# Attention layer: order of the value products, of the gate tiles' products, and of each attention tile's norm

## The chip, the cores and the metric

The kernel runs on one core of a Trainium2 chip. The metric is the device time of one execution in microseconds (us). Engines are named as in the profile: PE is TensorE (matmul), PEld its weight load, DVE is VectorE, ACT is ScalarE, POOL is GpSimd, SP the engine that issues most of the DMAs.

## The reference

One layer over 512 latent tokens and 256 context tokens, width 1024, in float32. Cut to what matters:

```
mod = silu(c) @ w_ada + b_ada                       # shifts, scales and gates, also for the context
h   = rms_norm(x) * (1 + sc1) + sh1                 # latent; hc likewise for the context
aq, ak, av, dq, dk, dv, dz, da, db, ga, gd = split_cols(h @ w_in)
q_a = axial_rope(rms_norm(heads(aq, 8), q_norm_g))  # 8 query heads, 2 key/value heads, 64 wide
k_a = axial_rope(rms_norm(heads(ak, 2), k_norm_g))
y_attn = softmax over (keys within 128 positions, all context keys, a sink logit) @ values
y_dn = gated DeltaNet in both directions, chunks of 64: a triangular solve per chunk, a scan over chunks
y = sigmoid(ga) * (y_attn @ w_br_attn) + sigmoid(gd) * (y_dn @ w_br_dn)
x = x + gt1 * (y @ w_out)
x = x + gt2 * (relu(norm2(x) @ w_mlp1) ** 2 @ w_mlp2)
```

## The kernel before

**Split products.** Every float32 operand of a large product is split into an upper part ("hi", rounded to fp32r) and a lower part ("lo", the rest). A product is the sum of three: hi x hi, hi x lo, lo x hi. A weight tile is 128 x 1024. `wload` fetches it into a buffer `wr` (four of them, DMA issued by SP at L250), makes `wh` with an ACT copy (L259) and `wl` in one of two ways: as a DVE subtract `wr - wh` (L266), or, with `late=True`, as an ACT copy of `-wh` (L263) followed by a DMA from POOL that adds the weight tile in memory to it (L264). There are two `wh` and two `wl` buffers, so a tile's `wh` can be written once the tile two before has had its last product with it. The queue `wq` lists the tiles in the order in which they are needed and `wnext()` hands out the next, loading one ahead.

**Order of the work.** The kernel is written with Python generators: `weave` takes steps from several of them in turn, by given shares. A scheduler then fixes one order of instructions for each engine ahead of the run; it may move an instruction past others that it doesn't depend on. During the run each engine works through its own row in order and waits by semaphores. Products accumulate in eight PSUM banks.

**Stages of this case.** Times in brackets are from the trace.

- *Attention tiles* (about 95 to 147 us). `attn_in` makes the tiles K, Q0, Q1, Q2, V, Q3. `in_tile_steps` multiplies: 16 products with `wh` (L424), for K and V another 16 of 256 columns for the context, then 8 with `wl` (L429), in steps of two k-tiles. When a tile is done it is finished: for K and Q `qk_norm` squares it (ACT L447), copies it (ACT L448), sums the squares by a product with a block matrix (PE L450), rotates (DVE L453 to L456), scales (L461), and the result is split (ACT L184, DVE L185; for K L485, L486). For V the tile is copied (ACT L495), transposed by PE (L499) and split. Woven with it are the first triangular solves: products L777, L802, L803, DVE operations L801 to L857, ACT copies L148.
- *Outputs* (185 to 295). `outputs` runs once for each query block and key/value head: for pairs of key blocks the probabilities are transposed on PE (L596), split into hi (ACT L184) and lo (DVE L185), and `values` multiplies them by the values on PE (L586), ended by ACT L610, DVE L611 and L618. `scores` runs ahead for later units: products L541 to L553, the maximum (DVE L554, L555) and the exponential (ACT L148). The remaining DeltaNet tiles (L424, L429, convolution L641 to L643) and the first three gate tiles (`ND1 = 3`, tiles `T_GD`) fill in.
- *Scans* (375 to 475, and some at 295 to 375). The DeltaNet scan over chunks is a chain of short products (PE L1152, L1164, L1185) and DVE operations (L1156, L1157, L1170, L1201). The remaining gate tiles (17) fill in: `gate_tiles` issues 24 products each (L1028), in groups of three for each k-tile: two with `wh`, one with `wl`. A gate ends with a tanh (ACT L148) and, for some, DVE L1033. DVE also has L1094 (another weight product), L1278, L1279 and L1285 (from the join of the solves) there.
- *The rest*: modulation and norms before 80 us, the output projection to 560 us, the MLP from 560 to 909 us (L317 to L319).

`combine` (L869) joins two half solves; it is called with a function that runs filling products between its two groups of matmuls.

Of the kernel before, what the change touches and what calls it, by code (L numbers as in the profile page):

```python
# [99 lines left out]
def tile_layer(ctx: ExitStack, tc: tile.TileContext, I: dict, out: bass.AP, dbg=None):  # L100
# [272 lines left out]
    for b in [wab_, xs_, cs_, rstd, scb]:  # L373
# [6 lines left out]
                                                        *range(T_DQ, T_DQ + 4))]  # L380
    wq += [(I["win"][t + i], KT) for t, i in gates[:ND1]]
    wq += [(I["wbr"][0, ct], 4) for ct in range(8)] + [(I["win"][t + i], KT) for t, i in gates[ND1:]]
# [92 lines left out]

    def k_attn():

        acc = yield from in_tile_steps(T_AK, True)
        t = qk_norm(acc[:, :512], SEQ, kg, True)
        t2 = qk_norm(acc[:, 512:768], CTX, kg)  # L480
        acc.free()
        for src, o in ((t[:, :512], slice(0, 512)), (t2[:, :CTX], slice(512, 768))):
            for kv, r in enumerate(own):
                for r2 in own:
                    A.activation(r32(KH[kv][r2, o]), src[r], AF.Copy)  # L485
                V.tensor_tensor(r32(KLo[kv][r, o]), src[r], KH[kv][r, o], op=ALU.subtract)  # L486
        t.free()
        t2.free()
        yield

    def v_attn():

        acc = yield from in_tile_steps(T_AV, True)
        raw = alloc(768)
# [11 lines left out]
        pt.free()  # L506
        yield

    def q_attn(j):
        acc = yield from in_tile_steps(T_AQ + j, False)  # L510
        t = qk_norm(acc.ap, SEQ, qgs, True)
        acc.free()
        src = t[:, :512].rearrange("p (b t) -> p b t", b=4)
        for kv, r in enumerate(own):
            split(src[r], Q[kv][r, :, j, :], Q[kv][own[1 - kv], :, j, :])
        t.free()
        yield

# [54 lines left out]
    def outputs(qb, kv):  # L573
# [7 lines left out]
        def values(at, ph, last):  # L581
            m = len(at)
            for x, i in enumerate(at):
                v = r32(VS[:, cols[i] * 256 + kv * P:cols[i] * 256 + (kv + 1) * P])
                for y, b in enumerate(ph):
                    PE.matmul(pv.ap, v, r32(b[:, x * 512:x * 512 + 512]), start=(i == y == 0),  # L586
# [281 lines left out]

    def combine(nto, XTf, XRf, XTb, XRb, XAf, XAb, inplace, between=lambda: None):  # L869

# [9 lines left out]
        Y.free()  # L880
        between()
        XO = bank()
# [8 lines left out]
        if not inplace:  # L891
            A.activation(XAf[:, :, :HC], XTf, AF.Copy)
            A.activation(XAb[:, :, :HC], XTb, AF.Copy)
        for a in range(2):
            lo, hi = quad(a, 0), quad(a, 1)
            A.activation(XAf[hi, :, HC:], XTf[hi], AF.Copy)
# [39 lines left out]
    def attn_in():  # L936
        yield from k_attn()
        for j in range(3):
            yield from q_attn(j)
        yield from v_attn()  # L940
        yield from q_attn(3)

# [61 lines left out]
    def combine0():  # L1004
# [7 lines left out]
        na, sw = v3(nat.ap), v3(swp.ap)  # L1012
        combine(NTO[0], na[:, :16], sw[:, :16], sw[:, 16:], na[:, 16:], v64(XA[0][0].ap), v64(XA[0][1].ap), False)
        nat.free()
# [6 lines left out]
    def gate_tiles(todo):  # L1021

        for kind, i in todo:
            w = wnext()
            acc = bank()
            for k in range(KT):
                for p, (x, y) in enumerate(((0, 0), (0, 1), (1, 0))):
                    PE.matmul(acc.ap, w[x][:, k, :], hx[k][y], start=(k == p == 0), stop=(k == KT - 1 and p == 2))  # L1028
                    yield
            if kind == T_GA:  # L1030
# [24 lines left out]
    for n, u in enumerate(units):  # L1055
        work = [(outputs(*u), (span(u[0])[2] + 3) // 2 + 1), (qts, QTS[n]), (inv, INV[3])]
        if n == CO:
            work.append((seq(combine0), 1))
        weave(*work, (ahead, 4))
# [198 lines left out]
    for g in range(2):  # L1258
        ms = slice(16 * g, 16 * g + 16)
        f, b = xa[0][:, ms], xa[1][:, ms]  # L1260
        run_fill(FILL[1] - CPAUSE)
        combine(NTO[1 + g], f[:, :, :HC], xr3[0][:, ms], b[:, :, :HC], xr3[1][:, ms], f, b, True, lambda: run_fill(CPAUSE))
        NTO[1 + g].free()
# [323 lines left out]
```

## Time and profile before

| | |
|---|---|
| median of 3 runs | 912.52 us (911.92 to 914.22) |
| profiled execution | 911.22 us, span 909.5 us |
| granted TensorE clock | 1.0 |
| busy: PE, PEld | 879.4, 704.7 us |
| busy: DVE, ACT, POOL | 585.4, 454.9, 25.2 us |

Each row of a timeline gives the start, the duration, the engine, the line and operation, what it writes and reads, and in brackets the idle time before it with what ended it. "ACT m L495" as a releaser is the ACT instruction of line L495 that wrote a tile m. A group row gives the busy time and the mean of one in ns, then the idle time of the engine in front of the group. Matmuls overlap, so the time from one start to the next, not the duration, is what a product takes of PE.

### The profile page before, as it was taken

What the parts mean: (1) busy time and instruction counts of PE and PEld (TensorE: products, weight loads), DVE (VectorE), ACT (ScalarE), POOL (GpSimd) and SP (SyncE); (2) the same over time, 40 slices, a digit from 0 to 9 for tenths busy, and PEclk for the clock granted to TensorE, in tenths of its full rate; (3) what the DMA queues carried; (4) which work ended last, traced back from release to release, by engine and by line L of the source; (5) the groups of instructions that cost most, each with busy time, mean ns of one, the idle gap of its engine ahead of it and who ended that gap; (6) DMA issues with size and microseconds to landing.
All of it is one profiled execution on the core that took longest, in us unless ns stands there. A gap on an engine that the chain in (4) does not pass through costs nothing.

```text
span 909.5 us, 16844 instructions
## 1 busy us (share of the span) xinstructions
PE 879.4 (97%) x7082; PEld 704.7 (77%) x7082; DVE 585.4 (64%) x999; ACT 454.9 (50%) x819; POOL 25.2 (3%) x40
## 2 busy tenths in 40 slices
PE   8999999999899999999999999999999999999998
PEld 5668777867677787777678789888888888888886
DVE  3578799887778997677867988941654335324511
ACT  6588755476568786465663445630452134113400
POOL 0010001010000002010000000000000000000000
PEclk9999999999999999999999999999999999999999
DMA  8671455533001133633316773640553224322111
GB/s 355 262 230 21 92 117 120 112 71 58 13 13 35 56 110 94 207 98 95 117 37 219 245 245 135 227 144 1 188 157 95 70 73 150 103 69 79 38 47 46
DMA packets 30460, 105.59 MB, mean 116 GB/s; under 512 B 3760, under 2 KB 4400, under 8 KB 29360
## 3 DMA queue, kind: packets, MB, share of 16 engines
q1 hardware_dynamic: 28368, 97.18, 33.1%
q0 software_dynamic: 2016, 7.34, 5.0%
q8 instruction: 55, 0.90, 0.4%
q14 instruction: 21, 0.17, 0.1%
HBM read 102.41 MB, written 2.10 MB: 115 GB/s over the span
## 4 chain that ended last, share of the span: by engine, by line
PE 80%; DVE 10%; ACT 5%; issue 2%; DMA 1%; SPq 0%; DVEq 0%; ACTq 0%
PE banks L319 16%; PE banks L317 16%; PE banks L318 16%; PE banks L1028 9%; PE banks L424 5%; PE banks L1073 2%; PE banks L429 2%; PE banks L586 2%; PE banks L596 1%; PE banks L1164 1%; ACT m L148 1%; PE banks L662 1%; PE banks L1185 1%; PE banks L1152 1%; PE banks L210 1%
## 5 line engine op out<-in xcount | busy, mean ns | idle before, releaser
L317 PE MATMUL banks<-m,m 128*128 128x512 f32 (+1 forms) x600 | 223.6, 377 | 2.6 <-DVE m L643 1.6
L318 PE MATMUL banks<-m,m 128*128 128x512 f32 (+1 forms) x600 | 224.5, 376 | 0.1
L319 PE MATMUL banks<-m,m 128*128 128x512 f32 (+1 forms) x600 | 224.2, 376 | 0.0
L259 ACT ACTIVATE m<-wr 128x1024 fp32r<-128x1024 f32 x68 | 71.8, 1059 | 155.1 <-PE banks L318 74.0
L317 PEld LDWEIGHTS banks<-m,m 128*128 128x128 f32 x600 | 111.8, 188 | 26.0 <-ACT m L323 2.8
L318 PEld LDWEIGHTS banks<-m,m 128*128 128x128 f32 x600 | 112.5, 188 | 21.9 <-DVE m L324 1.5
L319 PEld LDWEIGHTS banks<-m,m 128*128 128x128 f32 x600 | 112.4, 188 | 21.3 <-issue 1.2
L266 DVE TENSOR_TENSOR m<-wr,m 128x1024 fp32r<-128x1024 f32 x68 | 82.8, 1224 | 62.8 <-ACT m L259 31.2
L1028 PE MATMUL banks<-m,wh 128*128 128x512 f32 x320 | 104.5, 405 | 1.5 <-issue 0.8
L1471 DVE SCALAR_TENSOR_TENSOR m<-banks,modT,m 128x512 f32<-128x512 f32 x32 | 24.0, 750 | 105.3 <-PE banks L319 105.3
L259 ACT ACTIVATE wh<-wr 128x1024 fp32r<-128x1024 f32 (+1 forms) x58 | 54.6, 941 | 50.6 <-issue 11.4
L424 PE MATMUL banks<-m,wh 128*128 128x512 f32 (+1 forms) x320 | 75.9, 374 | 1.2 <-DVE m L823 1.2
L1028 PEld LDWEIGHTS banks<-m,wh 128*128 128x128 f32 x320 | 58.0, 188 | 14.2 <-issue 1.0
L1028 PE MATMUL banks<-m,wl 128*128 128x512 f32 x160 | 64.7, 405 | 0.0
L424 PEld LDWEIGHTS banks<-m,wh 128*128 128x128 f32 x320 | 53.0, 189 | 11.5 <-issue 1.9
L266 DVE TENSOR_TENSOR wl<-wr,wh 128x1024 fp32r<-128x1024 f32 (+1 forms) x44 | 45.2, 1028 | 16.6 <-ACT wh L259 16.5
L184 ACT ACTIVATE m<-m 128x512 fp32r<-128x512 f32 (+1 forms) x56 | 34.8, 629 | 38.1 <-DVE m L1454 21.5
L185 DVE TENSOR_TENSOR m<-m,m 128x512 fp32r<-128x512 f32 (+1 forms) x56 | 38.3, 689 | 21.6 <-ACT m L184 21.3
L1094 DVE SCALAR_TENSOR_TENSOR m<-wa,m 128x1024 f32<-128x1024 f32 x32 | 39.0, 1223 | 12.6 <-DMA wa<-in_wada 7.4
L317 PE MATMUL banks<-m,wh 128*128 128x512 f32 (+1 forms) x120 | 42.0, 352 | 0.0
L319 PE MATMUL banks<-m,wl 128*128 128x512 f32 (+1 forms) x120 | 42.0, 351 | 0.0
L318 PE MATMUL banks<-m,wh 128*128 128x512 f32 (+1 forms) x120 | 41.8, 349 | 0.0
(241 smaller groups left out, 1371.8 us busy)
## 6 DMA issues: line engine op xcount, KB each, us to landing
wr<-in_wm SPq DMA_DIRECT2D x64, 512.0 KB, 3.7
wr<-in_win SPq DMA_DIRECT2D x38, 512.0 KB, 3.7
wa<-in_wada SPq DMA_DIRECT2D x32, 512.0 KB, 4.1
m<-in_wada SPq DMA_DIRECT2D x8, 1024.0 KB, 12.3
wl<-in_win POOLq DMA_DIRECT2D x14, 512.0 KB, 5.7
m<-in_xT SPq DMA_DIRECT2D x8, 512.0 KB, 5.6
wr<-in_wbr SPq DMA_DIRECT2D x16, 256.0 KB, 2.6
wr<-in_wout SPq DMA_DIRECT2D x8, 512.0 KB, 4.6
```

Source lines behind the costliest of these rows:

```text
L184: A.activation(r32(hi), src, AF.Copy)
L185: (eng or V).tensor_tensor(r32(lo), src, hi, op=ALU.subtract)
L259: h = A.activation(r32(hi), raw, AF.Copy)
L266: V.tensor_tensor(r32(lo), raw, hi, op=ALU.subtract)
L317: PE.matmul(acc, w[0][:, k, :], xhi, start=(start and i == 0), stop=False)
L318: PE.matmul(acc, w[0][:, k, :], xlo, start=False, stop=False)
L319: PE.matmul(acc, w[1][:, k, :], xhi, start=False, stop=(stop and i == n - 1))
L424: PE.matmul(a, w[0][:, k, :], x, start=(k == 0 and x is xs[k][0]), stop=False)
L429: PE.matmul(a, w[1][:, k, :], xs[k][0], start=False, stop=(k == KT - 1))
L1028: PE.matmul(acc.ap, w[x][:, k, :], hx[k][y], start=(k == p == 0), stop=(k == KT - 1 and p == 2))
L1094: V.scalar_tensor_tensor(t.ap, wa, 0.5, scr.ap, op0=ALU.mult, op1=ALU.mult, accum_out=modT[:, grp, j:j + 1])
L1471: V.scalar_tensor_tensor(xn_[ct], acc.ap, modT[:, 3, ct:ct + 1], xn_[ct], op0=ALU.mult, op1=ALU.add)
```

## The change

Three things move; a fourth (`combine` turned into a generator, and called as such) only lets its second half be stepped, and both of its callers still run its work in the same order.

1. `values` loops over hi and lo outside and over the two key blocks inside: both upper products come first, then both lower ones.
2. The first three gate tiles are loaded with `late=True`, so that their `wl` comes from an ACT copy and an adding DMA instead of a DVE subtract. All 20 gate tiles issue their 16 products with `wh` first and then the 8 with `wl`.
3. `attn_in` takes the first step of the next tile (4 products, or 8 with the context) before it finishes a tile.

```
-    wq += [(I["win"][t + i], KT) for t, i in gates[:ND1]]
+    wq += [(I["win"][t + i], KT, None, None, True) for t, i in gates[:ND1]]
...
-    def k_attn():
-        acc = yield from in_tile_steps(T_AK, True)
+    def k_attn(acc):
...
         def values(at, ph, last):
             m = len(at)
-            for x, i in enumerate(at):
-                v = r32(VS[:, cols[i] * 256 + kv * P:cols[i] * 256 + (kv + 1) * P])
-                for y, b in enumerate(ph):
+            for y, b in enumerate(ph):
+                for x, i in enumerate(at):
+                    v = r32(VS[:, cols[i] * 256 + kv * P:cols[i] * 256 + (kv + 1) * P])
                     PE.matmul(pv.ap, v, r32(b[:, x * 512:x * 512 + 512]), start=(i == y == 0),
                               stop=(last and x == m - 1 and y == 1))
...
-    def combine(nto, XTf, XRf, XTb, XRb, XAf, XAb, inplace, between=lambda: None):
+    def combine(nto, XTf, XRf, XTb, XRb, XAf, XAb, inplace):
...
-        between()
+        yield
...
     def attn_in():
-        yield from k_attn()
-        for j in range(3):
-            yield from q_attn(j)
-        yield from v_attn()
-        yield from q_attn(3)
+        qs = [lambda acc, j=j: q_attn(acc, j) for j in range(4)]
+        todo = [(T_AK, k_attn)] + [(T_AQ + j, qs[j]) for j in range(3)] + [(T_AV, v_attn), (T_AQ + 3, qs[3])]
+        done = None
+        for ti, finish in todo:
+            g = in_tile_steps(ti, ti in (T_AK, T_AV))
+            while True:
+                try:
+                    next(g)
+                except StopIteration as e:
+                    acc = e.value
+                    break
+                if done:
+                    done[0](done[1])
+                done = None
+                yield
+            done = finish, acc
+            if ti == T_AQ + 3:
+                finish(acc)
+            yield
...
-            for k in range(KT):
-                for p, (x, y) in enumerate(((0, 0), (0, 1), (1, 0))):
-                    PE.matmul(acc.ap, w[x][:, k, :], hx[k][y], start=(k == p == 0), stop=(k == KT - 1 and p == 2))
-                    yield
+            for p, (x, y, k) in enumerate([(0, y, k) for k in range(KT) for y in range(2)] + [(1, 0, k) for k in range(KT)]):
+                PE.matmul(acc.ap, w[x][:, k, :], hx[k][y], start=(p == 0), stop=(p == 3 * KT - 1))
+                yield
```

Line numbers shift by up to 11 lines in the changed kernel. In the rows below, L496 is the old L499 (V's transposes), L492 the old L495 (V's copy), L580 the old L586 (value products), L590 the old L596 (transposes of the probabilities), L540 to L547 the old L546 to L553 (scores), L1042 the old L1033, L1289, L1290 and L1296 the old L1278, L1279 and L1285, L1165 and L1166 the old L1156 and L1157; the other names of the two rows pair up by operation.

**Attention tiles, ACT, from Q2's square on.** `wh_1313` is Q3's upper part before, `wh_1297` after; L447 and L448 work on Q2 (`m_1283`, then `m_1310`), L495 on V. Before:

```order
L447 ACTIVATE m_1283<-banks 128x512
L448 ACTIVATE m_1283<-banks,qgs 128x512
L263 ACTIVATE wl_1314<-wh_1313 128x1024
L148 ACTIVATE m_1283<-banks,epsc 128x512
L148 ACTIVATE m_1283<-m_1283 128x512
L259 ACTIVATE wh_1392<-wr_1390 128x1024
L184 ACTIVATE m_547<-m_1283 64x4x128
L184 ACTIVATE m_548<-m_1283 64x4x128
L495 ACTIVATE m_1378<-banks 128x768
L263 ACTIVATE wl_1393<-wh_1392 128x1024
```

After:

```order
L259 ACTIVATE wh_1297<-wr_1295 128x1024
L148 ACTIVATE m_759<-banks 128x512
L148 ACTIVATE m_760<-banks 128x512
L263 ACTIVATE wl_1298<-wh_1297 128x1024
L259 ACTIVATE wh_1380<-wr_1378 128x1024
L447 ACTIVATE m_1310<-banks 128x512
L448 ACTIVATE m_1310<-banks,qgs 128x512
L148 ACTIVATE m_1310<-banks,epsc 128x512
L148 ACTIVATE m_1310<-m_1310 128x512
L184 ACTIVATE m_547<-m_1310 64x4x128
L184 ACTIVATE m_548<-m_1310 64x4x128
L259 ACTIVATE wh_1452<-wr_1450 128x1024
```

The lower part's copy (L263) and the next tile's upper part (L259) now stand ahead of Q2's square. On PE, Q3's sixteen upper products come ahead of all of V's, and V's transposes (L499) move. Before, from V's last lower products on (`wh_1313` and `wl_1314` are Q3's):

```order
L429 MATMUL banks<-m_167,wl_1196 128x512
L429 MATMUL banks<-m_168,wl_1196 128x256
L424 MATMUL banks<-m_167,wh_1313 128x512 x7
L499 MATMUL banks<-c_ident,m_1378 128x128 x6
L424 MATMUL banks<-m_167,wh_1313 128x512 x9
L429 MATMUL banks<-m_167,wl_1314 128x512 x8
```

After, from V's last lower products on (`wl_1298` is Q3's, `wh_1380` the next tile's):

```order
L429 MATMUL banks<-m_167,wl_1180 128x512
L429 MATMUL banks<-m_168,wl_1180 128x256
L429 MATMUL banks<-m_167,wl_1298 128x512 x8
L424 MATMUL banks<-m_168,wh_1380 128x256
L496 MATMUL banks<-c_ident,m_1389 128x128 x6
L450 MATMUL banks<-m_1433,c_bones 128x512
```

The transposes stood behind the seventh of Q3's upper products; they now stand behind Q3's last lower one.

**Outputs, DVE, around the first gate tile's subtract.** `wl_2413` is that tile's lower part, `m_2365` the lower part of two blocks of probabilities, `m_2206` an output and `st_2256`, `st_2374` maxima. Before:

```order
L611 TENSOR_TENSOR m_2206<-m_2206,banks 64x512
L555 TENSOR_SCALAR st_2256<-st_2256,nsink 128x1
L266 TENSOR_TENSOR wl_2413<-wr_2410,wh_2412 128x1024
L618 TENSOR_TENSOR m_2206<-m_2206,banks 64x512
L564 TENSOR_TENSOR st_2256<-st_2256,nsink 128x4
L642 SCALAR_TENSOR_TENSOR m_2370<-banks,c_prm,m_2370 128x511
L554 TENSOR_REDUCE st_2374<-banks 128x1
L185 TENSOR_TENSOR m_548<-m_2206,m_547 128x512
L566 TENSOR_TENSOR st_2256<-st_2256 128x4
L185 TENSOR_TENSOR m_2365<-banks,m_2364 128x1024
L567 RECIPROCAL st_2256<-st_2256 128x4
L643 SCALAR_TENSOR_TENSOR m_2370<-banks,c_prm,m_2370 128x511
```

After, from the same operation on `m_2206` (L605 is the old L611):

```order
L605 TENSOR_TENSOR m_2206<-m_2206,banks 64x512
L612 TENSOR_TENSOR m_2206<-m_2206,banks 64x512
L548 TENSOR_REDUCE st_2256<-banks 128x1
L185 TENSOR_TENSOR m_548<-m_2206,m_547 128x512
L549 TENSOR_SCALAR st_2256<-st_2256,nsink 128x1
L636 SCALAR_TENSOR_TENSOR m_2370<-banks,c_prm,m_2370 128x511
L558 TENSOR_TENSOR st_2256<-st_2256,nsink 128x4
L548 TENSOR_REDUCE st_2374<-banks 128x1
L560 TENSOR_TENSOR st_2256<-st_2256 128x4
L637 SCALAR_TENSOR_TENSOR m_2370<-banks,c_prm,m_2370 128x511
L561 RECIPROCAL st_2256<-st_2256 128x4
L549 TENSOR_SCALAR st_2374<-st_2374,nsink 128x1
```

The subtract L266 is gone, and L643 (now L637) and two short operations on maxima (the reciprocal and one subtract, L567 and L555 before) have moved ahead of L185 on `m_2365` (the row after the last one shown). On PE, rows of scores (L540 to L547) and four transposes now stand between the upper and the lower products of these blocks:

```order
L580 MATMUL banks<-m_2364,m_553 128x512 x2
L542 MATMUL banks<-m_552,m_548 128x384
L545 LDWEIGHTS identb
L545 MATMUL banks<-maskb,identb 128x128
L547 LDWEIGHTS identb
L547 MATMUL banks<-maskb,identb 128x128
L590 MATMUL banks<-c_ident,m_2265 128x128 x2
L590 MATMUL banks<-c_ident,m_2324 128x128 x2
L540 MATMUL banks<-m_550,m_548 128x384
L580 MATMUL banks<-m_2365,m_553 128x512 x2
```

Here `m_2364` is the upper part and `m_2365` the lower; before, the four value products stood in one row, in the order upper, lower, upper, lower.

**Scans, DVE, from a gate tile's subtract to the scan's chain.** `wl_4202` is a gate tile's lower part. Before, from the row behind its subtract (then `wl_4199`) on:

```order
L1278 TENSOR_TENSOR m_3871<-m_758,banks 128x16x32
L1278 TENSOR_TENSOR m_3872<-m_759,banks 128x16x32
L1279 TENSOR_TENSOR m_760<-m_760,banks 128x512
L1285 COPY m_3871<-m_3871 32x16x32
L1285 COPY m_3872<-m_3872 32x16x32
L1285 COPY m_3871<-m_3871 32x16x32
L1285 COPY m_3872<-m_3872 32x16x32
L1156 TENSOR_TENSOR m_4171<-banks,eg 128x256
L1156 TENSOR_TENSOR m_4190<-banks,eg 128x256
L1157 SCALAR_TENSOR_TENSOR m_4171<-m_3130,m_4171 128x256
L1157 SCALAR_TENSOR_TENSOR m_4190<-m_3203,m_4190 128x256
L1033 SCALAR_TENSOR_TENSOR m_3246<-m_4193,m_3246 128x512
```

After:

```order
L266 TENSOR_TENSOR wl_4202<-wr_4199,wh_4201 128x1024
L1042 SCALAR_TENSOR_TENSOR m_3249<-m_4196,m_3249 128x512
L1289 TENSOR_TENSOR m_3874<-m_758,banks 128x16x32
L1289 TENSOR_TENSOR m_3875<-m_759,banks 128x16x32
L1290 TENSOR_TENSOR m_760<-m_760,banks 128x512
L1296 COPY m_3874<-m_3874 32x16x32
L1296 COPY m_3875<-m_3875 32x16x32
L1296 COPY m_3874<-m_3874 32x16x32
L1296 COPY m_3875<-m_3875 32x16x32
L1165 TENSOR_TENSOR m_4174<-banks,eg 128x256
L1165 TENSOR_TENSOR m_4193<-banks,eg 128x256
L1166 SCALAR_TENSOR_TENSOR m_4174<-m_3133,m_4174 128x256
```

The gate's L1033 (L1042), which stood behind the scan's L1157, now stands between the subtract and L1278 (L1289). The second L1166 follows in the next row.

More of the change, by code (lines that the diff above doesn't have):

```diff
@@ L488, in k_attn, with v_attn @@
         t2.free()
-        yield
-    def v_attn():
-        acc = yield from in_tile_steps(T_AV, True)
+    def v_attn(acc):
         raw = alloc(768)
@@ L506, in v_attn, with q_attn @@
         pt.free()
-        yield
-    def q_attn(j):
-        acc = yield from in_tile_steps(T_AQ + j, False)
+    def q_attn(acc, j):
         t = qk_norm(acc.ap, SEQ, qgs, True)
@@ L516, in q_attn @@
         t.free()
-        yield
     pkd = {}
@@ L1012, in combine0 @@
         na, sw = v3(nat.ap), v3(swp.ap)
-        combine(NTO[0], na[:, :16], sw[:, :16], sw[:, 16:], na[:, 16:], v64(XA[0][0].ap), v64(XA[0][1].ap), False)
+        yield
+        yield from combine(NTO[0], na[:, :16], sw[:, :16], sw[:, 16:], na[:, 16:], v64(XA[0][0].ap), v64(XA[0][1].ap), False)
         nat.free()
@@ L1025, in gate_tiles @@
             acc = bank()
-            for k in range(KT):
-                for p, (x, y) in enumerate(((0, 0), (0, 1), (1, 0))):
-                    PE.matmul(acc.ap, w[x][:, k, :], hx[k][y], start=(k == p == 0), stop=(k == KT - 1 and p == 2))
-                    yield
+            for p, (x, y, k) in enumerate([(0, y, k) for k in range(KT) for y in range(2)] + [(1, 0, k) for k in range(KT)]):
+                PE.matmul(acc.ap, w[x][:, k, :], hx[k][y], start=(p == 0), stop=(p == 3 * KT - 1))
+                yield
             if kind == T_GA:
@@ L1057, in tile_layer @@
         if n == CO:
-            work.append((seq(combine0), 1))
+            work.append((seq(lambda: list(combine0())), 1))
         weave(*work, (ahead, 4))
@@ L1261, in tile_layer @@
         run_fill(FILL[1] - CPAUSE)
-        combine(NTO[1 + g], f[:, :, :HC], xr3[0][:, ms], b[:, :, :HC], xr3[1][:, ms], f, b, True, lambda: run_fill(CPAUSE))
+        for n, _ in enumerate(combine(NTO[1 + g], f[:, :, :HC], xr3[0][:, ms], b[:, :, :HC], xr3[1][:, ms], f, b, True)):
+            if n == 0:
+                run_fill(CPAUSE)
         NTO[1 + g].free()
```

## The prediction

> **What bounds the kernel now.** I read the page first: busy shares and the chain that ended last.
>
> ```profile
> PE 879.4 (97%) x7082; PEld 704.7 (77%) x7082; DVE 585.4 (64%) x999; ACT 454.9 (50%) x819; POOL 25.2 (3%) x40
> PE 80%; DVE 10%; ACT 5%; issue 2%; DMA 1%; SPq 0%; DVEq 0%; ACTq 0%
> ```
>
> TensorE (PE) carries the time. No part of the change removes a product, so a gain can come only from holes in PE. Then the busy time by stage, for the stretches the change touches (length, then the busy time of PE, PEld, DVE, ACT and POOL):
>
> ```profile
> core 0: us, PE busy (x) PEld busy (x) DVE busy (x) ACT busy (x) POOL busy (x), PEclk, DMA share, GB/s
> ...
> 95.00:110.00 15.00, 14.32 (x238) 10.92 (x237) 12.82 (x24) 12.68 (x22) 1.73 (x2) 1.00 0.39 78
> 110.00:125.00 15.00, 14.42 (x179) 10.90 (x178) 14.91 (x26) 8.95 (x14) 0.86 (x1) 1.00 0.58 135
> 125.00:147.00 22.00, 19.80 (x96) 15.29 (x95) 21.26 (x43) 13.37 (x20) 1.73 (x2) 1.00 0.50 107
> ...
> 185.00:212.00 27.00, 24.55 (x376) 18.64 (x374) 19.57 (x35) 20.95 (x40) 2.95 (x5) 1.00 0.33 60
> 212.00:240.00 28.00, 25.99 (x155) 20.00 (x154) 20.96 (x36) 18.38 (x34) 0.86 (x1) 1.00 0.14 29
> 240.00:264.00 24.00, 21.83 (x127) 16.78 (x127) 18.29 (x35) 14.31 (x27) 0.00 (x0) 1.00 0.04 12
> 264.00:295.00 31.00, 29.80 (x167) 22.81 (x165) 25.16 (x46) 24.49 (x43) 0.00 (x0) 1.00 0.10 28
> ...
> 375.00:405.00 30.00, 27.50 (x526) 21.22 (x525) 21.34 (x39) 15.51 (x36) 2.97 (x4) 1.00 0.47 153
> 405.00:475.00 70.00, 66.22 (x1223) 51.39 (x1224) 49.93 (x112) 43.78 (x140) 0.00 (x0) 1.00 0.30 89
> ```
>
> PE idles 0.68 + 0.58 + 2.20 = 3.5 us in the attention tiles (95 to 147), 2.45 + 2.01 + 2.17 + 1.20 = 7.8 us in the outputs (185 to 295) and 2.50 + 3.78 = 6.3 us in the scans with gate tiles (375 to 475): 17.6 us in all, the ceiling of any gain. The clock was granted in full everywhere. Third, PE's waits say who ends these holes (total, times, longest):
>
> ```profile
> PE banks L1164 <- DVE m L1157: 3.9, 4, 1.7
> PE banks L586 <- DVE m L185: 2.3, 2, 2.1
> PE banks L596 <- ACT m L148: 2.3, 3, 0.8
> ...
> PE banks L424 <- DVE m L823: 1.2, 1, 1.2
> ...
> PE banks L499 <- ACT m L495: 1.0, 1, 1.0
> ...
> PE banks L596 <- DVE m L611: 0.7, 1, 0.7
> PE banks L450 <- ACT m L447: 0.7, 1, 0.7
> ```
>
> **The change part by part.**
>
> *Value products, and the subtract that leaves DVE* (outputs). The longest hole is a lower product that waits for its lower part. The two queues around it:
>
> ```profile
> 238.17 1.22 DVE L266 TENSOR_TENSOR wl<-wr,wh 128x1024 fp32r<-128x1024 f32 x1
> ...
> 242.43 1.22 DVE L185 TENSOR_TENSOR m<-banks,m 128x1024 fp32r<-128x1024 f32 x1
> ...
> 243.65 0.72 DVE L643 SCALAR_TENSOR_TENSOR m<-banks,c_prm,m 128x511 f32<-128x511 f32 x1
> ```
>
> ```profile
> 243.70 0.96 PE L586 MATMUL banks<-m,m 128*128 128x512 f32 x3 [2.09 <-DVE m L185]
> ...
> 244.68 0.60 PE L596 MATMUL banks<-c_ident,m 128*128 128x128 f32 x4
> ```
>
> The gate tile's subtract (L266, 1.22 us) stands in DVE's queue ahead of L185 and leaves it: -1.22. The new order puts L643 ahead of L185 instead: +0.72. On PE, a second upper product (0.23 us, below) and four transposes (0.60) now stand between the first upper product and the lower ones: -0.83. The 2.09 us become about 0.8, that is -1.3. The other 0.2 us of the L586 row lie at one lower product, which the second upper product covers: -0.2. L611 and its neighbour L618 move ahead of two reductions in DVE's order, which should shorten the 0.7-us wait for L611; I take -0.2. Sum -1.7. Bounds: all of L586's and L611's waits go (-3.0), or L643 and the later place of L185 cost their length with no cover gained (+0.9, L643 plus 0.2).
>
> *The three copies and adding transfers.* Added are three copies on ScalarE (ACT), three transfers of 512 KB issued by GpSimd, and the bytes they read. In the stretch with the outputs and first gate tiles (212 to 295), ACT's exponentials read:
>
> ```profile
> L148 ACT ACTIVATE m<-banks,st 128x640 f32<-128x640 f32 x13 | 10.3, 795 | 9.4 <-DVE st L555 8.8 <-PE banks L586 0.5
> ```
>
> ACT waited 8.8 us for DVE in front of 13 of them, 0.7 us each: a copy of 1.06 us (the row of 106.01 below has 1.08) fits in such a hole but for some 0.4 us. Of the three, one stands directly ahead of an exponential, the others ahead of a split or of L610. I take +0.4; bounds 0 and 3 x 1.06 = +3.2. GpSimd is idle there (0.00 busy from 240 to 295), nothing queues behind its issues, and the DMA engines are at 4 to 10%. The transfers must land before the 17th product of their tile:
>
> ```profile
> 273.92 1.06 ACT L259 ACTIVATE wh<-wr 128x1024 fp32r<-128x1024 f32 x1 [1.56 <-PE banks L1028]
> ...
> 281.25 0.40 PE L1028 MATMUL banks<-m,wh 128*128 128x512 f32 x1
> ```
>
> ```profile
> wl<-in_win POOLq DMA_DIRECT2D x14, 512.0 KB, 5.7
> ```
>
> The third tile is the tightest: upper part done at 275.0, copied by 276.1, landed near 281.8; its 17th product comes no earlier than 281.25 + 16 x 0.23 = 284.9. That 3.1 us is the cover; if the copy starts later than that, the excess is a hole in PE. I cost it at nothing.
>
> *Norms behind the next tile's first products* (attention tiles). The rows:
>
> ```profile
> 104.96 0.60 ACT L447 ACTIVATE m<-banks 128x512 f32<-128x512 f32 x1
> ...
> 106.01 1.08 ACT L263 ACTIVATE wl<-wh 128x1024 fp32r<-128x1024 f32 x1
> ```
>
> ```profile
> 139.33 0.81 ACT L495 ACTIVATE m<-banks 128x768 f32<-128x768 f32 x1
> ```
>
> ```profile
> 131.05 0.72 DVE L453 STREAM_SHUFFLE m<-m 128x512 f32<-128x512 f32 x1
> 131.66 0.68 DVE L823 TENSOR_TENSOR m<-m,banks 128x512 f32<-128x512 f32 x1
> ```
>
> V's transposes (L499) waited 1.0 us for the copy L495. Now Q3's eight lower products, 8 x 0.23 = 1.8 us, stand in front, more than L495's 0.81: -1.0. The norm sum of the first Q tile (L450) stands behind eight products of the next tile instead of four, 0.9 us more cover; but ACT now runs L263 (1.08) ahead of the square L447: the 0.7 us stay and grow by 0.2. V's products that waited 1.2 us for L823: the shuffle L453 is no longer ahead of L823, so it ends 0.6 earlier: -0.6. Q3's sixteen upper products take V's place ahead of that wait, an even exchange. Behind them the order hides a new wait: the copy L259 for the next tile waits for Q3's last upper product, and Q2's square stands behind it on ACT. L450 of Q2 comes ten products later on PE; I take +0.3, bounds 0 and 1.06 + 0.60 = 1.7. Sum -1.1. Bounds: all four waits go (-3.5), or none goes and the new one costs its full 1.7.
>
> *All gate tiles, upper products first* (scans). How the 1.7-us wait of L1164 arises:
>
> ```profile
> 393.25 1.06 ACT L259 ACTIVATE wh<-wr 128x1024 fp32r<-128x1024 f32 x1 [3.40 <-issue]
> 394.21 0.58 ACT L148 ACTIVATE m<-banks 128x512 f32<-128x512 f32 x1
> ```
>
> ```profile
> 394.34 1.23 DVE L266 TENSOR_TENSOR wl<-wr,wh 128x1024 fp32r<-128x1024 f32 x1 [2.44 <-ACT wh L259]
> 395.48 1.28 DVE L1278 TENSOR_TENSOR m<-m,banks 128x512 f32<-128x512 f32 x2
> ```
>
> ```profile
> 396.95 0.62 PE L1028 MATMUL banks<-m,wh 128*128 128x512 f32 x2
> 397.41 0.39 PE L1028 MATMUL banks<-m,wl 128*128 128x512 f32 x1
> ...
> 400.48 1.15 PE L1164 MATMUL banks<-m,m 64*64 64x64 f32 x32 [1.74 <-DVE m L1157]
> ```
>
> Two products take 0.46 us, so 0.23 each. The upper tile is released after the 16th product instead of the 23rd: 7 x 0.23 = 1.6 us earlier, and L259 and L266 can go up by as much. But the new order puts the gate's L1033 between L266 and L1278, and L1033 needs the tanh (L148) that ends at 394.8 in any case. At the usual 0.7 us of a 512-wide DVE operation (L823) L1278 would start near 395.4, as before. I take -0.2 here, and -0.4 for the three smaller waits of that row (2.2 us together). Sum -0.6. Bounds: all 3.9 us go, or one more 1.2-us DVE operation (a wide one such as L266's) lands between the operations that L1164 waits for: L1094 does so at one later place, +1.2.
>
> **Sum.** -1.7 + 0.4 - 1.1 - 0.6 = -3.0. The profiled execution took 911.22 us (span 909.5 and 1.7 around it), so 908.2. The median of the runs is 1.3 above the profiled execution, so 909.5.
>
> [...]
>
> **The rivals.**
>
> 1. More goes than I count: the earlier release reaches all four waits of L1164 (3.9 us), because L1033 finds its tanh ready. Then -3.9 in place of -0.6: 904.9, median 906.2. For it: L266 idled 2.44 us for the copy. Against it: the tanh's end. Chance 0.12.
>
> 2. L185 comes no earlier, because what moves into the subtract's place delays it as much, and the smaller gate terms don't come: the 1.2 us and the 0.6 us stay. 908.2 + 1.2 + 0.6 = 910.0, median 911.3, no change that can be told. For it: L643 and two short operations stand ahead of L185 at once. Against it: the lower products come 0.8 us later on PE as well. Chance 0.26.
>
> 3. Slower, by one mechanism: the copies ahead of the squares on ACT starve DVE in the attention tiles. From 110 to 125 DVE is busy 14.91 of 15 us, so a square that comes late leaves a hole nothing fills. Five tiles (K and Q0 to Q3) with 1.07 each are 5.3 us instead of -1.1: 908.2 + 6.4 = 914.6, median 915.9. It decides from the point where the squares end later than DVE's operations for the solves that can run meanwhile (up to L823). Against: DVE's order now puts such operations ahead of the norms. Chance 0.17.
>
> **How the numbers follow.** The forecast has 0.45; its own range is 907 to 911.5. Less than 0.3% (2.7 us, about what a measurement of this kernel can tell: the three runs spread over 0.25%) is no change, so faster means below 909.8. Of the forecast's 0.45 I put 0.36 there and 0.09 within. Faster 0.36 + 0.12 = 0.48; same 0.09 + 0.26 = 0.35; slower 0.17. The range runs from 904.5 (the first rival and somewhat more) to 915, just short of the third's full price.
>
> **What the profile after would show.** If right: no wait of L499 for L495 (new line numbers aside); L586's wait under 1.2 us; L424 waiting under 0.8 us for L823; no PE wait for a gate tile's lower part; DVE's gate subtracts three fewer. PE's idle time would fall to about 2.4 us in the attention tiles, 6.5 in the outputs and 5.7 in the scans. Wrong it is made by squares that start over 2 us later in the attention tiles, by exponentials that start right behind the new copies with PE waiting, or by L1164's waits above 5 us.

## The result, and the profile after

The changed kernel takes 906.36 us (median of 4 executions, 904.89 to 907.16), against 912.22 us for the kernel before in the same comparison: a ratio of 0.9923, 95% interval 0.9908 to 0.9939. The ratio corresponds to 7.0 us (5.6 to 8.4); the two medians lie 5.9 us apart, near the small end of that. The forecast was 909.5 us, a gain of 3.0. Direction and range held; the gain is about twice the forecast one. The profiled execution of the changed kernel took 907.16 us (span 905.4), the slowest of the four, and that of the kernel before (911.22 us) was faster than the four beside the changed kernel, so differences of the two traces (4 us) understate the gain.

The page of the changed kernel, busy shares and chain:

```profile
PE 880.2 (97%) x7082; PEld 707.0 (78%) x7082; DVE 581.5 (64%) x996; ACT 457.3 (51%) x822; POOL 27.7 (3%) x43
PE 83%; DVE 9%; ACT 4%; issue 2%; DMA 1%; SPq 0%; DVEq 0%; ACTq 0%
```

PE's work is the same, in a shorter span: holes went. DVE has three instructions fewer, ACT and POOL three more. Where the time went is read from four milestones, the first and last start of a line (columns: duration min/median/max in ns, first and last start in us). Before:

```profile
L777 PE MATMUL banks<-m x384: 216/216/241, 91.0 to 121.8; 64*32 64x64 f32 x192
```

```profile
L586 PE MATMUL banks<-m,m x72: 387/397/506, 187.8 to 284.6; 128*128 128x512 f32 x72
```

```profile
L1073 PE MATMUL banks<-m,wh x64: 390/393/797, 295.2 to 331.2; 128*128 128x512 f32 x64
```

```profile
L1164 PE MATMUL banks<-m,m x384: 218/218/267, 294.1 to 463.3; 64*64 64x64 f32 x192
```

After (the same lines, renumbered):

```profile
L771 PE MATMUL banks<-m x384: 216/216/240, 92.6 to 123.4; 64*32 64x64 f32 x192
```

```profile
L580 PE MATMUL banks<-m,m x72: 388/397/628, 189.1 to 285.0; 128*128 128x512 f32 x72
```

```profile
L1082 PE MATMUL banks<-m,wh x64: 387/393/797, 294.0 to 330.7; 128*128 128x512 f32 x64
```

```profile
L1173 PE MATMUL banks<-m,m x384: 218/218/267, 298.5 to 459.3; 64*64 64x64 f32 x192
```

The first solve product comes 1.6 us later: 0.8 of it is there from the first products of the modulation on, in rows that the change does not move, and 0.65 is a wait of PE for ACT at 77.6 us. From there to the first value product (the attention tiles) the new order saves 0.2 us (with the second decimal: 91.03 to 187.78 before, 92.56 to 189.12 after); to the first product of the attention's branch projection (the outputs) 2.6; to the scan's last product 2.8. What follows is equal. The stretches of the prediction, after:

```profile
core 0: us, PE busy (x) PEld busy (x) DVE busy (x) ACT busy (x) POOL busy (x), PEclk, DMA share, GB/s
...
95.00:110.00 15.00, 14.00 (x145) 9.97 (x137) 11.63 (x22) 13.50 (x25) 1.72 (x2) 1.00 0.38 75
110.00:125.00 15.00, 14.75 (x299) 11.39 (x299) 14.91 (x27) 8.12 (x13) 0.86 (x1) 1.00 0.63 138
125.00:147.00 22.00, 20.08 (x97) 15.66 (x97) 21.33 (x41) 13.66 (x20) 1.72 (x2) 1.00 0.40 98
...
185.00:212.00 27.00, 25.19 (x374) 18.55 (x373) 19.22 (x34) 19.80 (x38) 3.80 (x6) 1.00 0.32 71
212.00:240.00 28.00, 27.21 (x164) 21.39 (x162) 21.05 (x38) 18.30 (x34) 0.86 (x1) 1.00 0.17 38
240.00:264.00 24.00, 21.93 (x122) 17.35 (x121) 17.06 (x34) 14.85 (x29) 0.86 (x1) 0.93 0.18 34
264.00:295.00 31.00, 30.50 (x160) 23.89 (x158) 24.82 (x47) 26.58 (x49) 1.72 (x2) 1.00 0.30 55
...
375.00:405.00 30.00, 28.27 (x560) 22.18 (x559) 21.45 (x40) 15.95 (x33) 2.89 (x4) 1.00 0.44 137
405.00:475.00 70.00, 68.00 (x1208) 52.83 (x1207) 53.58 (x116) 45.08 (x142) 0.00 (x0) 1.00 0.30 89
```

PE's idle time is 3.2 us in the attention tiles (3.5 before), 5.2 in the outputs (7.8) and 3.7 in the scans (6.3). The stretch from 240 has a granted clock of 0.93, which before had 1.00. PE's waits after:

```profile
PE banks L1173 <- DVE m L1166: 2.8, 3, 1.7
PE banks L590 <- ACT m L148: 2.6, 2, 2.1
PE banks L450 <- ACT m L447: 1.9, 3, 1.0
...
PE banks L424 <- DVE m L817: 1.3, 1, 1.3
...
PE banks L580 <- DVE m L185: 0.7, 2, 0.4
```

The 2.1-us wait for a lower part of probabilities is gone, and a wait of the same length has come within 3 us of its place: PE's transposes (L590) for an exponential (ACT L148). The timeline there, DVE, ACT and PE:

```profile
240.79 0.20 DVE L549 TENSOR_SCALAR st<-st,nsink 128x1 f32<-128x1 f32 x1
```

```profile
240.49 1.04 ACT L263 ACTIVATE wl<-wh 128x1024 fp32r<-128x1024 f32 x1
241.43 0.78 ACT L148 ACTIVATE m<-banks,st 128x640 f32<-128x640 f32 x1
```

```profile
242.36 2.39 PE L590 MATMUL banks<-c_ident,m 128*128 128x128 f32 x10 [2.07 <-ACT m L148]
```

The exponential's maximum was ready at 241.0, and the added copy L263 held ACT until 241.4: 0.4 us of this hole is the price of the copy, as the forecast took it for all three. The rest of the hole is not the copy's: the kernel with the value products' order and the norms' new place but without these copies (below) has 1.69 us at the same place. So the largest hole of the outputs kept its length and changed its cause. PE's waits in that stage fell from 7.3 to 4.7 us in sum: for lower parts (value products) from 2.3 to 0.7 us and the smaller ones from 2.7 to 1.4, while the transposes' waits for exponentials rose from 2.3 to 2.6.

### The profile page after: what moved, and what is told of

Same layout as the page of the kernel before. It is cut to its first block, busy times and chain, and to the rows that moved or that the text cites. A ratio compares the mean times of both kernels' runs of the same rounds, so it can differ in the third digit from the quotient of the medians.

```text
span 905.4 us, 16846 instructions
## 1 busy us (share of the span) xinstructions
PE 880.2 (97%) x7082; PEld 707.0 (78%) x7082; DVE 581.5 (64%) x996; ACT 457.3 (51%) x822; POOL 27.7 (3%) x43
## 4 chain that ended last, share of the span: by engine, by line
PE 83%; DVE 9%; ACT 4%; issue 2%; DMA 1%; SPq 0%; DVEq 0%; ACTq 0%
PE banks L317 16%; PE banks L318 16%; PE banks L319 16%; PE banks L1037 12%; PE banks L424 5%; PE banks L1082 3%; PE banks L429 2%; PE banks L580 2%; PE banks L1173 1%; PE banks L590 1%; PE banks L656 1%; PE banks L1194 1%; DVE m L185 1%; PE banks L1161 1%; DMA m<-in_xT 1%
## 5 line engine op out<-in xcount | busy, mean ns | idle before, releaser
L259 ACT ACTIVATE m<-wr 128x1024 fp32r<-128x1024 f32 x68 | 71.7, 1058 | 154.8 <-PE banks L318 77.4
L266 DVE TENSOR_TENSOR m<-wr,m 128x1024 fp32r<-128x1024 f32 x68 | 82.8, 1223 | 63.0 <-PE banks L318 34.2
L1037 PE MATMUL banks<-m,wh 128*128 128x512 f32 x320 | 85.6, 405 | 0.5 <-issue 0.5
L424 PE MATMUL banks<-m,wh 128*128 128x512 f32 (+1 forms) x320 | 74.0, 372 | 1.3 <-DVE m L817 1.3
L259 ACT ACTIVATE wh<-wr 128x1024 fp32r<-128x1024 f32 (+1 forms) x58 | 54.5, 940 | 40.9 <-PE banks L1037 11.2
L424 PEld LDWEIGHTS banks<-m,wh 128*128 128x128 f32 x320 | 52.9, 189 | 11.6 <-DVE m L817 1.7
L185 DVE TENSOR_TENSOR m<-m,m 128x512 fp32r<-128x512 f32 (+1 forms) x56 | 38.2, 689 | 21.8 <-ACT m L184 21.4
L266 DVE TENSOR_TENSOR wl<-wr,wh 128x1024 fp32r<-128x1024 f32 (+1 forms) x41 | 41.5, 1013 | 10.2 <-PE banks L1037 7.7
L1037 PE MATMUL banks<-m,wl 128*128 128x512 f32 x160 | 43.9, 402 | 0.0
```

Of the source, the lines that this page charges most:

```text
L185: (eng or V).tensor_tensor(r32(lo), src, hi, op=ALU.subtract)
L259: h = A.activation(r32(hi), raw, AF.Copy)
L266: V.tensor_tensor(r32(lo), raw, hi, op=ALU.subtract)
L424: PE.matmul(a, w[0][:, k, :], x, start=(k == 0 and x is xs[k][0]), stop=False)
L1037: PE.matmul(acc.ap, w[x][:, k, :], hx[k][y], start=(p == 0), stop=(p == 3 * KT - 1))
```

## The experiments

Times are medians; ratios are to the kernel before, run on the same chip in the same comparison, and differences in us follow from the ratio. Stage times in the table below come from milestones like those above, in one profiled execution each.

**Each part alone.** Value products:

```
-            for x, i in enumerate(at):
-                v = ...
-                for y, b in enumerate(ph):
+            for y, b in enumerate(ph):
+                for x, i in enumerate(at):
+                    v = ...
```

> Before with the value products' order alone (upper parts first). Theory A (the scans' gain comes from the gate tiles' order, the outputs' gain from the value products): 1 to 2 us faster than before, with the 2.1-us wait of the value products for DVE's lower parts under 1.2 us; nothing changes after 300 us. Rival B (what helps is the subtract that leaves DVE): no change, under 0.5 us, and the 2.1-us wait stays above 1.7 us.

Measured: 914.78 us, ratio 1.0019 (1.0004 to 1.0034). Slower, against both expectations, though the interval begins close to 1. In its profile L586 waits 3.4 us for DVE, not 2.3:

```profile
PE banks L586 <- DVE m L185: 3.4, 3, 1.6
```

Order in the 20 gate tiles:

```
-            for k in range(KT):
-                for p, (x, y) in enumerate(((0, 0), (0, 1), (1, 0))):
+            for p, (x, y, k) in enumerate([(0, y, k) for k in range(KT) for y in range(2)] + [(1, 0, k) for k in range(KT)]):
```

> Before with the order inside the 20 gate tiles alone (16 products with the upper part, then 8 with the lower). Theory A: 2.5 to 4 us faster, nearly all of it between 375 and 475 us, since the upper weight tile is released 1.6 us earlier and the waits of the scan's products and of the gate tiles' first products shrink from about 6 to below 4 us. Rival B: under 1 us, since the scan's chain waits for DVE and not for weights.

Measured: 909.86 us, ratio 0.9962 (0.9946 to 0.9978): 3.5 us faster, as theory A has it. But its reason is not seen: between 372 and 482 us the scan's products wait as long for DVE as before.

```profile
PE banks L1163 <- DVE m L1156: 3.8, 4, 1.7
```

What is gone in that stretch are two waits of the gate tiles' own first products, which the kernel before shows there:

```profile
PE banks L1028 <- issue: 0.8, 1, 0.8
...
PE banks L1028 <- ACT m L148: 0.7, 1, 0.7
```

Adding loads for the first three gate tiles:

```
-    wq += [(I["win"][t + i], KT) for t, i in gates[:ND1]]
+    wq += [(I["win"][t + i], KT, None, None, True) for t, i in gates[:ND1]]
```

> Before with the first three gate tiles' lower parts by ACT copy and adding DMA alone (the interleaved product order stays, so that a lower part is needed at the third product of its tile). Theory A: about no change (minus 1 to plus 1 us): DVE loses 3.7 us of work and the 2.1-us wait shrinks by up to 1.2, but the third tile's lower part lands up to 3 us late for its third product. Rival B: 2 to 3 us faster in the outputs.

Measured: 910.21 us, ratio 0.9968 (0.9954 to 0.9981): 2.9 us faster, so rival B. The 2.09-us wait for the lower part shrank to a quarter. In DVE's queue the subtract is gone, L643 now stands ahead of L185 and a 0.8-us reduction (L554) behind it. No product waits for an adding load even in the interleaved order:

```profile
243.29 0.97 PE L586 MATMUL banks<-m,m 128*128 128x512 f32 x3 [0.54 <-DVE m L185]
```

Norms behind the next tile's first products (the diff's `attn_in`, `k_attn`, `q_attn`, `v_attn`):

```
-        yield from k_attn()
-        for j in range(3):
-            yield from q_attn(j)
...
+                if done:
+                    done[0](done[1])
+                done = None
```

> Before with the attention tiles' norms behind the next tile's first products alone. Theory A: no change (minus 0.7 to plus 0.7 us): in the changed kernel the stretch from the first solve products to the first value product became only 0.2 us shorter. Rival C (the attention part gains and a slow start of the profiled execution hid it): 1 to 1.5 us faster.

Measured: 915.21 us, ratio 1.0015 (1.0001 to 1.0028): a little slower, as neither expectation has it, and barely clear of noise. The attention tiles themselves got 0.2 us shorter; in the profiled execution, which at 918.65 us was the slowest of the twelve, the loss is in stages that this part does not touch. A good part of it there is clock (see the table below).

**Parts left out of the whole.** The two gate parts without the other two:

```
-    wq += [(I["win"][t + i], KT) for t, i in gates[:ND1]]
+    wq += [(I["win"][t + i], KT, None, None, True) for t, i in gates[:ND1]]
...
-                for p, (x, y) in enumerate(((0, 0), (0, 1), (1, 0))):
+            for p, (x, y, k) in enumerate([(0, y, k) for k in range(KT) for y in range(2)] + [(1, 0, k) for k in range(KT)]):
```

> Before with the gate tiles' order and the adding loads, without the value products' order and without the norms' new place. The single parts measured 3.5 us faster (order in gate tiles), 2.9 us faster (adding loads), 1.7 us slower (value products) and 1.4 us slower (norms) than before, each in its own schedule. Theory A (the two gate parts carry the whole gain and add up; the other two bring nothing): 6 to 7 us faster than before, as the whole change. Rival D (the other two cost something beside these as well): 8 to 9.5 us faster, so better than the whole change. Rival E (the two gate parts overlap, and the other two parts help once these are in): under 5 us faster.

Measured: 906.08 us, ratio 0.9925 (0.9911 to 0.9939): the whole gain. Theory A.

From the whole change, `values` put back:

```
-            for y, b in enumerate(ph):
-                for x, i in enumerate(at):
+            for x, i in enumerate(at):
+                for y, b in enumerate(ph):
```

> The whole change without the value products' new order. Theory A: as the whole change within 0.7 us (7 us faster than before). Rival D: 1.7 us faster than the whole change, 8.7 than before. Rival E: at most 6 us faster than before, because upper products first help where the subtract has left DVE.

Measured: 910.4 us, ratio 0.9966 (0.9953 to 0.9979). Rival E's number: by these ratios, without the value products' order the whole loses 3.9 us of its 7. A hole in the outputs is back, 2.5 us long:

```profile
244.14 0.41 PE L540 MATMUL banks<-m,m 128*128 128x384 f32 x1 [2.48 <-DVE st L558]
```

From the whole change, `attn_in` and the tiles' finish put back:

```
-            done = finish, acc
...
+        yield from k_attn()
+        for j in range(3):
+            yield from q_attn(j)
```

> The whole change with the norms in their old place. Theory A: as the whole change within 0.7 us (7 us faster than before). Rival D: 1.4 us faster than the whole change, 8.4 than before. Rival E: at most 6 us faster than before.

Measured: 910.15 us, ratio 0.9962 (0.9949 to 0.9975), again rival E's number: 3.5 us lost. Together with the run before it this fits none of the three theories: values and norms each cost some 3.5 us beside the gate parts, and both together nothing. A part of these 3.5 us is clock: the two kernels had a mean granted clock of 0.9967 and 0.9970, against 0.9992 with the gate parts alone. At the 0.6 to 0.9 us for each 0.001 that the last section works out, that is 1.3 to 2.3 us.

From the whole change, the gate tiles interleaved again:

```
-            for p, (x, y, k) in enumerate([(0, y, k) for k in range(KT) for y in range(2)] + [(1, 0, k) for k in range(KT)]):
+            for k in range(KT):
+                for p, (x, y) in enumerate(((0, 0), (0, 1), (1, 0))):
```

> The whole change with the old interleaved order inside the gate tiles (the adding loads stay, so a lower part is needed at the third product). Theory A: the 3.5 us of the gate tiles' order are lost: 3 to 4 us faster than before. If the order only serves to cover the late lower parts of the first three tiles, PE shows waits for an adding load (wl from the weights in memory) of over 1 us between 260 and 295 us, and the kernel is under 2 us faster than before.

Measured: 908.46 us, ratio 0.9945 (0.9931 to 0.9958): 5 us faster than before, so the gate tiles' order is worth 2 us here by the two ratios, not 3.5. No product waits for an adding load, so it does not serve to cover them.

**Mechanisms.** Lower part first in the gate tiles:

```
-            for k in range(KT):
-                for p, (x, y) in enumerate(((0, 0), (0, 1), (1, 0))):
+            for p, (x, y, k) in enumerate([(1, 0, k) for k in range(KT)] + [(0, y, k) for k in range(KT) for y in range(2)]):
```

> Before with each gate tile's products in the order lower part first (8), then the 16 with the upper part: the upper tile is released at the end of its tile as before, the lower one 16 products earlier. Upper part first measured 3.5 us faster. Theory A (the earlier release of the upper weight tile is the cause): no gain, between 1 us faster and 2 us slower, and the scan's products wait for DVE as before (3.9 us or more). Rival F (any order that keeps products of one kind together, or the schedule that follows from it, gains): 3 us faster again.

Measured: 910.61 us, ratio 0.9973 (0.9961 to 0.9985): 2.5 us faster, though the upper tile is now released last. So rival F: the earlier release of the upper tile is not needed for most of the gain. By the medians it could explain about 1 us of the 3.5; the two intervals overlap, so even that is not shown. The scan's products wait less for DVE than before, against theory A, although here nothing about the upper tile comes earlier:

```profile
PE banks L1163 <- DVE m L1156: 2.8, 3, 1.4
```

The first three gate tiles without lower parts (their products with the lower part use the upper one):

```
+        if nolo:
+            return r32(hi), r32(hi)
```

> Before with the first three gate tiles' lower parts left out: their products with the lower part use the upper part, so three DVE subtracts of 1.22 us are gone and no copy and no adding load comes in their place. The adding loads measured 2.9 us faster. Theory G (the subtract was in the way on DVE, and the copies cost nothing): 2.5 to 3.5 us faster. Rival H (the copies cost on ACT in front of the exponentials): 4 us faster or more. Rival I (the subtract was not in the way; the gain comes from elsewhere in the schedule): under 1.5 us faster.

Measured: 909.78 us, ratio 0.9962 (0.995 to 0.9974): 3.5 us faster. Theory G: the subtracts were in the way. The copies and loads that replace them cost 0.0006 of 913 us, 0.5 us, by these ratios, which the intervals do not separate from nothing. The same 0.54-us remainder stands in the same place:

```profile
243.71 0.98 PE L588 MATMUL banks<-m,m 128*128 128x512 f32 x3 [0.54 <-DVE m L185]
```

Values and norms without the gate parts:

```
-            for x, i in enumerate(at):
+            for y, b in enumerate(ph):
...
-        yield from k_attn()
+        for ti, finish in todo:
```

> Before with the value products' order and the norms' new place together, without the two gate parts. Each alone measured 1.7 and 1.4 us slower; beside both gate parts each alone costs 3.5 to 3.9 us, and the two together 0. Theory J (the pair cancels by itself, since the norms' new place shifts the outputs' queues into a form that suits upper products first): within 1 us of before. Rival K (the two add up, and the cancelling needs the gate parts): 2.5 to 4 us slower.

Measured: 909.4 us, ratio 0.9963 (0.995 to 0.9977): 3.4 us faster, where each alone is slower. Neither theory has it. Its hole in the outputs is 1.69 us:

```profile
241.37 0.88 PE L590 MATMUL banks<-c_ident,m 128*128 128x128 f32 x6 [1.69 <-ACT m L148]
```

Adding loads for all 20 gate tiles, on top of the two gate parts:

```
-    wq += ... [(I["win"][t + i], KT) for t, i in gates[ND1:]]
+    wq += ... [(I["win"][t + i], KT, None, None, True) for t, i in gates[ND1:]]
```

> Both gate parts (906.1 us) with the adding load for all 20 gate tiles instead of three: 17 more DVE subtracts of 1.22 us give way to ACT copies of 1.06 us and 8.9 MB more transfers, in the scans, where PE waits 3.8 us in all for the scan's DVE operations that stand behind such subtracts. Theory A: 1 to 3 us faster than with three adding loads, with the scan's waits for DVE under 2 us. Rival H (the copies come in front of what ACT does for the scan, or the loads land late, since only one tile of lead is there): 1 to 4 us slower, with PE waiting for adding loads.

Measured: 913.57 us, ratio 0.9997 (0.9983 to 1.0012): all of the gain is lost, beyond rival H's price. A product waits for an adding load, and a solve product idles PE for 3 us at a place where the trace names no releaser:

```profile
337.73 0.50 PE L1027 MATMUL banks<-m,wl 128*128 128x512 f32 x1 [1.97 <-DMA wl<-in_win]
```

```profile
371.50 0.21 PE L878 MATMUL banks<-m,m 32*32 32x32 f32 x1 [3.02 <-issue]
```

Behind each of these two holes the granted clock falls, 1.7 us lost each time: it reads 0.84 and 0.82 in the two stretches of 5 us from 335 us on, 0.75 and 0.91 in those from 370 us on. So three tiles is not a size to be raised to 20; nothing between was run. The likely reason, not tested apart: the first three are loaded into a stretch where GpSimd idles (0.86 of 83 us busy) and the DMA engines are at 4 to 14% (212 to 295 us of the kernel before), the others into one where these are at 30 to 47% before any transfer is added.

**All together** (us against the kernel before, minus is faster; the stage columns from one profiled execution each, so with whatever clock it was granted; "falls" counts how often in that execution the granted clock fell, in the outputs and in the scans; the mean granted clock is over all executions of that kernel):

| kernel | parts | whole | outputs | scans | falls | mean clock |
|---|---|---|---|---|---|---|
| e1 | values | +1.7 | +4.5 | +1.5 | 3, 1 | 0.9967 |
| e4 | norms | +1.4 | +3.3 | +2.7 | 2, 1 | 0.9957 |
| e11 | values, norms | -3.4 | -2.4 | -0.4 | 0, 0 | 0.9988 |
| e2 | gate order | -3.5 | +0.7 | -2.7 | 1, 0 | 0.9966 |
| e8 | gate order, lower first | -2.5 | +0.1 | -3.2 | 0, 0 | 0.9968 |
| e3 | adding loads | -2.9 | -3.3 | +1.0 | 0, 0 | 0.9978 |
| e9 | three subtracts out | -3.5 | -2.8 | +0.9 | 0, 0 | 0.9992 |
| e7 | gate order, adding loads | -6.8 | -3.4 | -1.9 | 0, 0 | 0.9992 |
| u1 | all but values | -3.1 | +2.1 | -3.3 | 1, 0 | 0.9967 |
| u4 | all but norms | -3.5 | 0.0 | -1.0 | 1, 1 | 0.9970 |
| u2 | all but gate order | -5.0 | -3.5 | -0.7 | 0, 0 | 0.9980 |
| after | all | -7.0 | -2.6 | -2.8 | 1, 0 | 0.9985 |
| e12 | e7, 20 adding loads | -0.3 | -3.5 | +5.8 | 0, 2 | 0.9962 |

The kernel before had 0.9971 to 0.9976 beside them, and no fall in these stages of its profiled execution. Each fall loses 1.7 us of full clock, as the last section adds up, so by that estimate it lengthens a stage by up to 1.7 us; the falls are to be taken off before stages are compared. PE's idle time in a stage, from milestone to milestone, is the other measure; products that take longer add nothing to it.

Two effects are regular. In the scans PE idles 4.1 to 5.6 us in every kernel with the gate tiles grouped by part, 5.9 to 8.1 in the others (6.4 before); only e12, with 9.7, stands out. In the outputs it idles 5.2 to 5.5 us in every kernel that has the adding loads (or leaves the subtracts out) and does not have exactly one of values and norms, and also in e11, which has both of these alone; 7.5 to 8.4 in the others (7.9 before).

So values and norms do not help singly, and together they do. That they hurt singly is seen in the outputs only beside the adding loads (u1 8.4, u4 7.5, against 5.4 in e7). Without the gate parts the outputs of e1 and e4 idle 7.7 and 8.2 us, as before: the 4.5 and 3.3 us that they lost there in these executions go with three and two falls of the clock. Over all their executions the two were 1.7 and 1.4 us slower, with intervals that begin at 0.4 and 0.1 us, and at 0.6 to 0.9 us for each 0.001 of mean clock 0.2 to 0.4 and 0.8 to 1.3 of that is clock. Why the pair differs from its parts is not shown; the scheduler makes another order of the outputs for each, and one part changes rows of all engines there, well beyond the lines it edits.

## Why the prediction was right or wrong

- *Direction and range*: right. What bounded the kernel, PE with 17.6 us of holes in three stages, is where the gain came from: 5.5 us of holes less (17.6 to 12.1). The size was about half of what was measured, and the sum came that near partly by luck: the attention tiles gave 0.9 us less than their term, outputs and copies together 1.3 more, the scans 2.2 more. The idle times show it: 3.2, 5.2 and 3.7 us, where 2.4, 6.5 and 5.7 were forecast.
- *Attention tiles, -1.1*: got -0.2 by the milestones, -0.3 by the waits. V's transposes no longer wait for their copy, as worked out (-1.0). Two terms were mis-sized: L424 waits 1.3 us for L823 (now L817) and not 0.6, so the -0.6 did not come: the shuffle did leave DVE's queue ahead of it, but a 2.10-us transpose (L827, at 128.35) took a place there that before had its turn by 126.6 (L833); and L450 waits 1.9 us in three places, not 0.7 + 0.2 + 0.3 = 1.2. A wait of L777 for L823 (0.6 us) that I had not counted is gone. -1.0 - 0.6 + 1.2 + 0.1 = -0.3.
- *Outputs, -1.7 + 0.4*: got -2.6, in an execution that lost clock there. That the subtract's place in DVE's queue matters was right: with no change to the value products, e3 and e9 show the 2.09 us falling to 0.54, so it was worth 1.55 us at that place (ahead of it a wait of 0.84 us went as well and one of 0.78 came) and some 3 us in the stage. L643 stands ahead of L185 in e3 too, but there the reduction L554 went behind it in exchange, which it did not in the changed kernel. The forecast's term for the value products (their 0.83 us of cover) is not confirmed: alone they do not shorten the stage. And the hole itself was forecast to shrink to 0.8 us; in the changed kernel another of 2.07 us came in its place, with an exponential as its cause, and the gain lies in smaller waits. The second rival, that the subtract did not matter, is refuted by e3 and e9.
- *Copies and loads, +0.4*: about right. One copy costs 0.4 us in front of an exponential; e9 against e3 gives 0.5 for all three with their loads, not separated from nothing. One sign of being wrong did appear, an exponential right behind a new copy with PE waiting, but only 0.4 of its 2.07 us is the copy's. No product waited for a load.
- *Scans, -0.6*: got -2.8. This is the worst step: I counted only the four waits of L1164 and let the tanh eat most of it. Those waits did shrink by 1.1 us only (3.9 to 2.8), but not for the reason given: with the gate tiles' order alone (e2) they stay at 3.8, with both gate parts (e7) at 4.0, and with the upper tile released last (e8) they are 2.8. That this part of the number is near is luck. What I left out are waits of the gate tiles' own first products, 0.7 and 0.8 us, of which 0.5 is left, and smaller ones.
- *First rival* (906.2, the release reaches all four waits): its number is the measured one, its mechanism is not. e8 releases the upper tile last and still gains 2.5 of e2's 3.5 us. Why grouping by part shortens the scans stays open: with the lower products first or last the scheduler also orders the scans' other work anew, and no run held that fixed.
- *Third rival* (squares behind copies starve DVE): DVE stayed at 14.91 of 15 us from 110 to 125, so the price was not paid.
- *Share of time or place in a queue*: DVE was busy 20.96 of 28 us where the first subtract stood (212 to 240 us), and taking three subtracts off it gave 2.9 us (e3): a queue that was a quarter idle was still late where it counted.

## What to carry to other kernels

Ask of a moved instruction what stands behind it in its queue at the one place where another engine idles, not how busy its engine is; three subtracts of 1.2 us were worth 3 us there. A term worked out for one edit does not add to that of another when a scheduler orders the program anew each time: two edits that cost 1.4 and 1.7 us alone gave 3.4 us together, so combinations are to be measured, and a gain of a whole change is not evidence for each part of it. Before stages of two executions are compared, look at the clock of each: a fall of 1.7 us here is as large as the effects that were looked for. Two of the four parts (order in the gate tiles, adding loads for three tiles) give what the whole gives; nothing measured here beats the changed kernel.

## What the runs showed of the hardware

The 2.07-us hole of the changed kernel cost more than its length in the profiled execution, it seems. Behind it the granted clock falls (columns as in the stretches above):

```profile
240.00:243.00 3.00, 0.93 (x7) 0.76 (x6) 2.97 (x8) 2.40 (x6) 0.86 (x1) 0.88 0.01 3
243.00:246.00 3.00, 3.00 (x15) 2.65 (x14) 1.82 (x5) 2.73 (x4) 0.00 (x0) 0.55 0.86 132
246.00:249.00 3.00, 3.00 (x20) 2.62 (x18) 2.55 (x4) 0.60 (x1) 0.00 (x0) 1.00 0.22 42
```

That is 0.12 and 0.45 of 3 us, 1.7 us. In stretches of half a microsecond the clock reads 0.50 from 242.5 to 245.5, 1.00 up to 242.0 and again from 246.0, so by the 1.7 us lost it is at half for 3.4 us. All 14 falls of the table lose as much, 1.70 us each, added up from the clock of the one or two stretches of 5 us that hold a fall (here 0.73 and 0.93 from 240 to 250 us). The outputs as a whole (185 to 295 us), before, then with the value products alone, then with the two gate parts:

```profile
185.00:295.00 110.00, 102.18 (x820) 78.23 (x818) 83.99 (x150) 78.14 (x142) 3.81 (x6) 1.00 0.15 33
```

```profile
185.00:295.00 110.00, 103.25 (x787) 79.07 (x786) 79.30 (x141) 72.96 (x133) 3.80 (x6) 0.95 0.15 32
```

```profile
185.00:295.00 110.00, 104.19 (x814) 79.53 (x813) 83.45 (x154) 82.83 (x152) 6.62 (x10) 1.00 0.25 49
```

With the value products alone PE has no more holes than before, and yet the stage was 4.5 us longer in that execution: the clock of 0.95 is 5.5 of 110 us, three falls. Ahead of each of the 14 falls PE idled 1.3 to 3.0 of the last 4 us; but holes of 2.1 us without a fall are there too (the kernel before, e8, u2). Over 31 executions of the kernel before, the time rose by 0.6 us for each 0.001 of mean clock lost. The two gate parts (e7), whose holes near 240 us are 0.78 and 0.54 us long, had 0.9992 on average against 0.9974 for the kernel before beside it: 1.1 us of the gain of 6.8 at that slope, 1.6 at the 0.9 us that 0.001 of a 905-us span is by arithmetic. That a hole causes the fall is argued from where the falls stand; no run added a hole or filled one to show it, and the longest hole of the outputs does not order the kernels: e11 had a mean clock of 0.9988 with 1.69 us, e1 0.9967 with 1.57.
